# Forgetting attention: high probabilities by high, ones and low values in one 129-column product

## The chip, the core and the metric

The kernel runs on one core of a Trainium2 chip. The core has a matrix engine (TensorE, PE in the profile), a vector engine (VectorE, DVE), a scalar engine (ScalarE, ACT), GpSimd (POOL) and a sync engine (SP) that issues DMAs. The metric is the device time of one execution in microseconds, the median over several runs. Each profile is one execution, recorded by the hardware profiler.

## The reference

One decoder layer over 2048 positions of width 1024. Two mixers share a normalised input and one input projection: forgetting attention (8 heads of 64) and a sliding-window attention. Their gated outputs go through one output projection, a norm and a residual. What the change touches is the last line of the forgetting attention:

```python
def one_block(args):
    qb, cb, n = args
    s = jnp.einsum('bhqd,bhkd->bhqk', qb, kh, preferred_element_type=jnp.float32) * scale
    s = s + cb[..., None] - cum[:, :, None, :]
    ...
    s = jnp.where(causal, s, -jnp.inf)
    p = jax.nn.softmax(s, axis=-1)
    return jnp.einsum('bhqk,bhkd->bhqd', p.astype(vh.dtype), vh)
```

All of it is float32. The kernel reaches that accuracy with float16 products by splitting numbers into a high part and a low part, each float16. A product of two split numbers is then three matmuls: high by high, high by low, low by high.

## The kernel before

**Stages.** First the modulation, the norm, the transposition of the input and the sliding-window mixer with their projections (to about 480 us of the span). Then the forgetting attention (about 480 to 1025 us), with the remaining projections and, in its last head, the first part of the output projection between its steps. Then the rest of the output projection.

**Steps of the forgetting attention.** For each of 8 heads (`hd`) the queries are taken in 4 chunks of 512 (`ci`), and for each chunk the keys in pairs of 128-blocks up to the diagonal. One pair is a `Step`; there are 2, 4, 6 and 8 of them for the four chunks, 20 a head, 160 in all. A step has these parts, each a method:

- `scores` (L1286): PE computes the transposed scores of both key blocks into the PSUM tile `sta`, of which there is one buffer (`ps_st`, L1153). Two matmuls to each block (L1294, L1295), one more on the diagonal (L1297).
- `exp32` (L1299): ACT takes the exponential of `sta` to float32 (L1301).
- `high` (L1303): ACT copies that to float16, the high part of the probabilities (L1305).
- `low` (L1307): DVE subtracts, which gives the low part (L1308).
- `pv` (L1310): PE multiplies probabilities by values into the PSUM tile `poa`, of which there is one buffer (`ps_po`, L1154). For each key block and each 128-query block `u` at or below the diagonal there are three matmuls with the probabilities as weights: high by high values and ones (65 columns, L1318), high by low values (64 columns, L1320), low by high values and ones (65 columns, L1321). The values lie in `vt` as 64 high columns, a column of ones, and 64 low columns (`VW` = 129). The column of ones yields the sum of the probabilities. All of a chunk's steps accumulate in one `poa`.
- With the chunk's last step, `pv` ends in an eviction, 32 in all: DVE takes the reciprocal of the sums (L1325), multiplies (L1327), and SP's queue stores the result to DRAM (`o_d`, L1328), from where the output projection loads it in the last head.

**Order.** It is written out by hand in the loop at L1575 to L1636, and each engine's queue runs in that order. Step s issues its exponential, the low part of step s−1, the first half of other work (`todo`), its high part, the scores of step s+1, then `pv` of step s−2 (`PV_LAG` = 2), and the second half of other work. That other work is projections (L317 in units of three 512-column matmuls), and row maxima for the next head: PE computes scores again (L1245) into one of five rotating PSUM banks `bk`, and DVE reduces them (L1248, on the diagonal L1250). Some of it is put off by a tick or more (`after`), such as ACT's evictions of projections (L361, L1028) and DVE's gate multiply (L357). Splits of weights into high and low (L255 on ACT, L261 on DVE) run there too.

In particular ACT's queue has, in this order around an eviction: the high part of step s, then the exponential of step s+1. DVE's queue has the work ticked off in step s, the eviction's two instructions, then row maxima and the low part of step s.

Elsewhere in the kernel, L335 multiplies the input by value weights in 128-column matmuls with a weight load each, L340 and L767 are ACT's evictions of values from PSUM, L771 is DVE's.

Of the kernel before, what the change touches and what calls it, by code (L numbers as in the profile page):

```python
# [10 lines left out]
F32 = mybir.dt.float32  # L11
# [3 lines left out]
AF = mybir.ActivationFunctionType  # L15
ALU = mybir.AluOpType
AX = mybir.AxisListType

P = 128
# [12 lines left out]
LIFT_A = 3.0 * math.log(2.0)  # L32
XA, XB, XC = 2.0 ** 15, 2.0 ** 6, 2.0 ** -5
XM, XR, VW = 66, 69, 129
LW = 72
TWO_PI = 2.0 * math.pi
OFF_QA, OFF_KA, OFF_VA, OFF_FA, OFF_ZA = 0, 512, 1024, 1536, 1544
# [4 lines left out]
def hybrid_layer(  # L42
# [17 lines left out]
    V, A, G, PE, SP = nc.vector, nc.scalar, nc.gpsimd, nc.tensor, nc.sync  # L60
# [20 lines left out]
    def sm(n, tag):  # L81
        return small.tile([P, n], F32, tag=tag, name=tag)
# [97 lines left out]
    def bank(hold=False):  # L180
        n = next(n for n in order_ if n not in held)
        order_.remove(n)
        order_.append(n)
        if hold:
            held.add(n)
        return n
# [241 lines left out]
    start = ExitStack()  # L428
# [229 lines left out]
    def open_fox():  # L658
# [5 lines left out]
        vt = fx["vt"] = fxv.tile([P, NB, 8, VW], F16, name="vt")  # L664
        fx["lk"] = fxv.tile([P, LW], F16, name="lk")
        fx["lq"] = [fxv.tile([P, LW], F16, name=f"lq{n}") for n in range(2)]
        fx["cst"] = cst = fxv.tile([P, XR], F16, name="cst")
# [169 lines left out]
    class Pair:  # L837
# [62 lines left out]
        def pv(self):  # L900
            j, i = self.j, self.i
            po = ps_pv.tile([P, 4, 64], F32, tag="pv", name="pob")
            for e, (i_, k0, nk) in enumerate(self.blocks):
                for h in range(2):
                    for b in range(nk):
                        for n, (pp_, vv) in enumerate(((0, 0), (0, 1), (1, 0))):
                            PE.matmul(po[:, 2 * e + h, :], self.ptt[:, pp_, self.at[e] + h * nk + b, :],  # L907
                                      vb[:, k0 + b, self.g, 64 * vv:64 * vv + 64],
                                      start=(b == 0 and n == 0), stop=(b == nk - 1 and n == 2))

            def out_():
                on = onp.tile([P, 2, P], F32, tag="on", name="on")
                V.tensor_tensor(on[:].rearrange("p e (h d) -> p (e h) d", h=2), po[:],
                                self.rinv[:].unsqueeze(2).broadcast_to([P, 4, 64]), op=ALU.mult)
                G.dma_start(o_d[i // 4][(i % 4) * P:(i % 4 + 2) * P, (4 + j) * P:(5 + j) * P]
                            .rearrange("(e p) c -> p e c", p=P), on[:])

            after(1, out_)
# [231 lines left out]
    def fox_pool(name, bufs, **kw):  # L1150
        return fox.enter_context(tc.tile_pool(name=name, bufs=bufs, reuse_waits="tile", **kw))

    ps_st = fox_pool("ps_st", 1, space=PSUM)  # L1153
    ps_po = fox_pool("ps_po", 1, space=PSUM)  # L1154
# [44 lines left out]
    def ext_rows(cols, w, places):  # L1199

        px = bk[bank()][:]
        PE.matmul(px[0:LW, 0:P], cols, identh[:], start=True, stop=True)
        rw = fxr.tile([48, P], F16, tag="rw", name="rw")
# [8 lines left out]
    vt, lk, lq = fx["vt"], fx["lk"], fx["lq"]  # L1212
# [63 lines left out]
    class Step:  # L1276
# [33 lines left out]
        def pv(self):  # L1310
            hd, ph = self.hd, self.ph
            if self.first:
                self.po_[0] = ps_po.tile([P, 4, 65], F32, tag="po", name="poa")
            po = self.po_[0]
            for n, (b, u0, o) in enumerate(self.blocks):
                for u in range(u0, 4):
                    pq = slice(o + (u - u0) * P, o + (u - u0 + 1) * P)
                    PE.matmul(po[:, u, :], ph[:, 0, pq], vt[:, b, hd, 0:65],  # L1318
                              start=(self.first and n == 0 and u == 0), stop=False)
                    PE.matmul(po[:, u, 0:64], ph[:, 0, pq], vt[:, b, hd, 65:VW], start=False, stop=False)  # L1320
                    PE.matmul(po[:, u, :], ph[:, 1, pq], vt[:, b, hd, 0:65], start=False,  # L1321
                              stop=(self.last and n == len(self.blocks) - 1))
            if self.last:
                rinv = sm(4, "a_ri")
                V.reciprocal(rinv[:], po[:, :, 64])  # L1325
                on = op_.tile([P, 4, 64], F32, tag="ona", name="ona")
                V.tensor_tensor(on[:], po[:, :, 0:64], rinv[:].unsqueeze(2).broadcast_to([P, 4, 64]), op=ALU.mult)  # L1327
                SP.dma_start(o_d[self.ci][:, hd * 64:(hd + 1) * 64].rearrange("(u p) d -> p u d", p=P), on[:])  # L1328

        po_ = {}  # L1330
# [213 lines left out]
    with tc.manual_schedule():  # L1544
# [30 lines left out]
        for s, stp_ in enumerate(steps):  # L1575
            hd, r = divmod(s, NS)
# [105 lines left out]
```

## Time and profile before

| what | value |
|---|---|
| median of 3 runs | 1194.2 us (1192.35 to 1195.01) |
| span of the profiled execution, first to last instruction | 1188.7 us |
| mean granted PE clock in it | 0.993 |
| PE busy | 1147.3 us, 97% of the span |
| DVE busy | 914.1 us, 77% |
| ACT busy | 665.9 us, 56% |
| probabilities by values, three matmuls | 1088 each |
| evictions of it (reciprocal, multiply) | 32 each |

The profiled execution is a separate one from the timed runs; of its time the span is what the profile shows, and it lies 5.5 us below the median.

How to read the profile: an engine's busy time is the time in which at least one of its instructions runs. Matmuls are pipelined, so their busy times overlap and the mean duration of one is not the distance between two. A group's row gives source line, engine, operation, output and inputs, shape and count, then busy time in us, the mean duration of one in ns, then the engine's idle time just before its instructions, and what ended it. A timeline row gives the start in us from the span's start, the duration in us, the instruction, and in brackets the engine's idle time before it with what ended that.

### The profile page before, as it was taken

The numbers are of one execution on the slowest core, as the hardware profiler recorded it, in microseconds if no ns is written. First come the engines' busy times: TensorE is split into PE (matmuls) and PEld (weight loads), VectorE is DVE, ScalarE is ACT, GpSimd is POOL, SyncE is SP. The second block draws the span as 40 slices with busy tenths as digits, with TensorE's granted clock in tenths as the row PEclk, the third lists the DMA queues.
The fourth block names the chain that finished last, engine by engine and source line by source line (L and its number), as shares of the span: only waits on it lengthen the run. The fifth ranks groups of instructions, "written<-read, shape, count | busy, mean of one in ns | idle before, by whom it ended". The sixth has DMA issues, their size and how long they took to land.

```text
span 1188.7 us, 27244 instructions
## 1 busy us (share of the span) xinstructions
PE 1147.3 (97%) x10853; PEld 693.6 (58%) x10853; DVE 914.1 (77%) x2263; ACT 665.9 (56%) x1102; POOL 115.2 (10%) x231
## 2 busy tenths in 40 slices
PE   5899999999999998999999999999999999999997
PEld 2475556765558976555555555555555555555554
DVE  7876678687776748688888889887888887766665
ACT  2784345464655521476766667666666778433332
POOL 2000112212121211001000101001000000000000
PEclk9899999999999999999999999999999999999999
DMA  9745433314223322413325322212311345455642
GB/s 333 277 121 87 84 89 99 61 59 109 83 70 88 58 63 63 65 50 95 68 70 72 102 63 60 50 48 71 48 42 39 92 127 176 147 171 184 198 167 96
DMA packets 87579, 120.22 MB, mean 101 GB/s; under 512 B 27508, under 2 KB 63388, under 8 KB 87452
## 3 DMA queue, kind: packets, MB, share of 16 engines
q1 hardware_dynamic: 76184, 85.69, 24.4%
q0 software_dynamic: 10832, 32.50, 13.2%
q8 instruction: 85, 1.39, 0.6%
q14 instruction: 42, 0.34, 0.1%
q10 hardware_dynamic: 436, 0.28, 0.1%
HBM read 71.04 MB, written 25.18 MB: 81 GB/s over the span
## 4 chain that ended last, share of the span: by engine, by line
PE 79%; DVE 10%; DMA 6%; issue 2%; ACT 2%; SPq 1%; DVEq 0%; ACTq 0%
PE bk L317 29%; PE bk L1489 13%; PE bk L335 7%; PE sta L1295 4%; PE sta L1294 4%; PE bk L1245 4%; PE poa L1320 2%; PE poa L1321 2%; PE poa L1318 2%; DMA wa<-in_w_ada_dram 2%; PE pxb L888 2%; PE pss L855 2%; PE pob L907 2%; DVE a_m L1248 1%; PE bk L1410 1%
## 5 line engine op out<-in xcount | busy, mean ns | idle before, releaser
L1301 ACT ACTIVATE p<-sta,lift,scl_qk 128x1024 f32<-128x1024 f32 (+2 forms) x160 | 172.0, 1075 | 143.7 <-PE sta L1295 88.2
L317 PE MATMUL bk<-hT,wh_qk 128*128 128x512 f16 x768 | 195.3, 380 | 0.0
L1248 DVE TENSOR_REDUCE a_m<-bk 128x1 f32<-128x512 f32 x192 | 130.5, 686 | 55.2 <-PE bk L1245 54.0
L1308 DVE TENSOR_TENSOR pha<-p,pha 128x1024 f16<-128x1024 f32 (+2 forms) x160 | 169.1, 1057 | 0.2 <-ACT pha L1305 0.2
L1489 PE MATMUL bk<-wohl,oz 128*128 128x512 f16 x744 | 167.0, 379 | 0.7 <-DVE oz L1438 0.7
L1305 ACT ACTIVATE pha<-p 128x1024 f16<-128x1024 f32 (+2 forms) x160 | 148.1, 926 | 5.4 <-PE poa L1321 0.7
L1489 PEld LDWEIGHTS <-oz 128*128 128x128 f16 x744 | 71.9, 99 | 79.4 <-DVE oz L1438 2.8
L317 PEld LDWEIGHTS <-wh_qk 128*128 128x128 f16 x768 | 72.5, 98 | 78.2 <-issue 6.6
L1321 PE MATMUL poa<-vt,pha 128*128 128x65 f16 x1088 | 116.1, 192 | 1.4 <-DVE pha L1308 1.2
L1318 PE MATMUL poa<-vt,pha 128*128 128x65 f16 x1088 | 116.5, 193 | 0.5 <-DVE ona L1327 0.4
L1320 PE MATMUL poa<-vt,pha 128*128 128x64 f16 x1088 | 116.5, 194 | 0.0
L1245 PE MATMUL bk<-T 66*128 66x512 f16 (+2 forms) x320 | 110.2, 350 | 3.1 <-DVE a_m L1248 3.0
L1294 PE MATMUL sta<-T 128*128 128x512 f16 (+1 forms) x320 | 110.9, 346 | 2.5 <-ACT p L1301 2.4
L1318 PEld LDWEIGHTS <-pha 128*128 128x128 f16 x1088 | 101.5, 96 | 15.1 <-DVE ona L1327 1.5
L1295 PE MATMUL sta<-T 69*128 69x512 f16 (+1 forms) x320 | 109.8, 348 | 0.0
L1320 PEld LDWEIGHTS <-pha 128*128 128x128 f16 x1088 | 100.9, 97 | 11.4
L1321 PEld LDWEIGHTS <-pha 128*128 128x128 f16 x1088 | 100.8, 99 | 1.8 <-DVE pha L1308 1.7
L317 PE MATMUL bk<-hT,wh_za 128*128 128x512 f16 x384 | 99.7, 378 | 0.0
L335 PE MATMUL bk<-wh_va,hT 128*128 128x128 f16 x1536 | 90.7, 219 | 0.0
L335 PEld LDWEIGHTS <-hT 128*128 128x128 f16 x1536 | 87.5, 98 | 4.7 <-issue 2.1
L317 PE MATMUL bk<-hT,wh_zb 128*128 128x512 f16 x384 | 88.9, 379 | 0.0
L317 PE MATMUL bk<-hT,wh_qb 128*128 128x512 f16 x384 | 87.4, 379 | 0.0
(498 smaller groups left out, 1860.4 us busy)
## 6 DMA issues: line engine op xcount, KB each, us to landing
hT<-in_x_dram SPq DMA_DIRECT2D x20, 512.0 KB
wa<-in_w_ada_dram SPq DMA_DIRECT2D x16, 512.0 KB
z_d<-tz POOLq DMA_DIRECT2D x32, 256.0 KB, 2.9
T<-stq SPq DMA_DIRECT2D x64, 128.0 KB
T<-o_d SPq DMA_DIRECT2D x16, 512.0 KB
T<-z_d SPq DMA_DIRECT2D x16, 512.0 KB
out_dram<-hT SPq DMA_DIRECT2D x15, 512.0 KB
xt<-in_x_dram SPq DMA_DIRECT2D x12, 512.0 KB
```

The costliest lines, as they stand in the source:

```text
L317: PE.matmul(ps, whl[:, a, k, :], hT[ci][:, b, k, :], start=(k == 0 and n == 0), stop=(k == KT - 1 and n == 2))
L335: PE.matmul(ps[:, u * P:(u + 1) * P], hT[ci][:, a, k, u * P:(u + 1) * P], whl[:, b, k, :], start=(k == 0 and n == 0), stop=(k == KT - 1 an ...
L1245: PE.matmul(mx[:, :w], T[0:XM, 0, i * P:(i + 1) * P], T[0:XM, 2, pc * CH:pc * CH + w], start=True, stop=True)
L1294: PE.matmul(self.st[:, o:o + w], T[:, 3, kb_], T[:, 1, qc], start=True, stop=False)
L1295: PE.matmul(self.st[:, o:o + w], T[0:XR, 2, kb_], T[0:XR, 0, qc], start=False, stop=not diag)
L1301: A.activation(self.p32[:, :self.w], self.st[:, :self.w], AF.Exp, scale=scl[f"qk{self.hd}"][:], bias=lift[:])
L1305: A.activation(self.ph[:, 0, :self.w], self.p32[:, :self.w], AF.Copy)
L1308: V.tensor_tensor(self.ph[:, 1, :self.w], self.p32[:, :self.w], self.ph[:, 0, :self.w], op=ALU.subtract)
L1318: PE.matmul(po[:, u, :], ph[:, 0, pq], vt[:, b, hd, 0:65], start=(self.first and n == 0 and u == 0), stop=False)
L1320: PE.matmul(po[:, u, 0:64], ph[:, 0, pq], vt[:, b, hd, 65:VW], start=False, stop=False)
L1321: PE.matmul(po[:, u, :], ph[:, 1, pq], vt[:, b, hd, 0:65], start=False, stop=(self.last and n == len(self.blocks) - 1))
L1489: PE.matmul(py, self.hl[:, i, k, :], w_slot(8 * j + k)[:, cc], start=(k == 0 and m_ == 0), stop=(k == KT - 1 and m_ == 2))
```

## The change

For query blocks `u` = 0, 1, 2 the products of the high probabilities with the high values and ones and with the low values become one product of 129 columns, which leaves its low 64 columns in columns of their own; block 3 keeps its three products. The PSUM tile grows from 260 to 452 float32 columns (three times 129 and 65), within one bank. At the eviction ACT copies the low columns of three blocks to SBUF, DVE adds the high columns to them, multiplies block 3 out of PSUM, and multiplies the three others in SBUF.

```diff
--- before.py
+++ after.py
@@ -32,6 +32,7 @@
 LIFT_A = 3.0 * math.log(2.0)
 XA, XB, XC = 2.0 ** 15, 2.0 ** 6, 2.0 ** -5
 XM, XR, VW = 66, 69, 129
+PO_W = 3 * VW + 65
 LW = 72
 TWO_PI = 2.0 * math.pi
 OFF_QA, OFF_KA, OFF_VA, OFF_FA, OFF_ZA = 0, 512, 1024, 1536, 1544
@@ -1310,21 +1311,28 @@
         def pv(self):
             hd, ph = self.hd, self.ph
             if self.first:
-                self.po_[0] = ps_po.tile([P, 4, 65], F32, tag="po", name="poa")
+                self.po_[0] = ps_po.tile([P, PO_W], F32, tag="po", name="poa")
             po = self.po_[0]
             for n, (b, u0, o) in enumerate(self.blocks):
                 for u in range(u0, 4):
                     pq = slice(o + (u - u0) * P, o + (u - u0 + 1) * P)
-                    PE.matmul(po[:, u, :], ph[:, 0, pq], vt[:, b, hd, 0:65],
+                    c = u * VW
+                    w = VW if u < 3 else 65
+                    PE.matmul(po[:, c:c + w], ph[:, 0, pq], vt[:, b, hd, 0:w],
                               start=(self.first and n == 0 and u == 0), stop=False)
-                    PE.matmul(po[:, u, 0:64], ph[:, 0, pq], vt[:, b, hd, 65:VW], start=False, stop=False)
-                    PE.matmul(po[:, u, :], ph[:, 1, pq], vt[:, b, hd, 0:65], start=False,
+                    if u == 3:
+                        PE.matmul(po[:, c:c + 64], ph[:, 0, pq], vt[:, b, hd, 65:VW], start=False, stop=False)
+                    PE.matmul(po[:, c:c + 65], ph[:, 1, pq], vt[:, b, hd, 0:65], start=False,
                               stop=(self.last and n == len(self.blocks) - 1))
             if self.last:
                 rinv = sm(4, "a_ri")
-                V.reciprocal(rinv[:], po[:, :, 64])
+                V.reciprocal(rinv[:], po[:, 64:PO_W:VW])
                 on = op_.tile([P, 4, 64], F32, tag="ona", name="ona")
-                V.tensor_tensor(on[:], po[:, :, 0:64], rinv[:].unsqueeze(2).broadcast_to([P, 4, 64]), op=ALU.mult)
+                p3 = po[:, 0:3 * VW].rearrange("p (u c) -> p u c", u=3)
+                A.activation(on[:, 0:3], p3[:, :, 65:VW], AF.Copy)
+                V.tensor_tensor(on[:, 0:3], p3[:, :, 0:64], on[:, 0:3], op=ALU.add)
+                V.tensor_scalar(on[:, 3], po[:, 3 * VW:3 * VW + 64], rinv[:, 3:4], None, op0=ALU.mult)
+                V.tensor_tensor(on[:, 0:3], on[:, 0:3], rinv[:, 0:3].unsqueeze(2).broadcast_to([P, 3, 64]), op=ALU.mult)
                 SP.dma_start(o_d[self.ci][:, hd * 64:(hd + 1) * 64].rearrange("(u p) d -> p u d", p=P), on[:])
 
         po_ = {}
```

## The prediction, made before the changed kernel ran

> **What bounds the kernel now.** I read the page first.
>
> ```profile
> span 1188.7 us, 27244 instructions
> PE 1147.3 (97%) x10853; PEld 693.6 (58%) x10853; DVE 914.1 (77%) x2263; ACT 665.9 (56%) x1102; POOL 115.2 (10%) x231
> PE 79%; DVE 10%; DMA 6%; issue 2%; ACT 2%; SPq 1%; DVEq 0%; ACTq 0%
> ```
>
> TensorE (PE) is busy 97% of the span and holds 79% of the chain that ended last. The change touches only the forgetting-attention steps, which run from about 480 to 1025 us, so I asked for that stage in windows. The columns are window, its length, and the busy time of PE, PE's weight loads, VectorE (DVE), ScalarE (ACT) and GpSimd, then the granted clock.
>
> ```profile
> 500.00:600.00 100.00, 99.60 (x1043) 58.13 (x1042) 87.74 (x202) 69.29 (x81) 8.64 (x14) 1.00 0.35 81
> 700.00:800.00 100.00, 99.35 (x1013) 57.48 (x1011) 87.95 (x201) 67.57 (x78) 7.26 (x12) 1.00 0.25 59
> 900.00:1000.00 100.00, 95.90 (x1041) 57.20 (x1040) 83.27 (x166) 77.51 (x97) 1.63 (x3) 1.00 0.38 114
> ```
>
> PE hardly rests, at full clock. DVE is the second engine, 83 to 88% busy; ACT has a quarter to a third of its time free. So in this stage a nanosecond taken from PE counts, and any wait put in front of PE counts too. What PE waits for today stands in the groups of instructions (busy total, mean ns, then the idle time before them and who ended it):
>
> ```profile
> L1294 PE MATMUL sta<-T 128*128 128x512 f16 (+1 forms) x320 | 110.9, 346 | 2.5 <-ACT p L1301 2.4
> L1245 PE MATMUL bk<-T 66*128 66x512 f16 (+2 forms) x320 | 110.2, 350 | 3.1 <-DVE a_m L1248 3.0
> L1318 PE MATMUL poa<-vt,pha 128*128 128x65 f16 x1088 | 116.5, 193 | 0.5 <-DVE ona L1327 0.4
> L1321 PE MATMUL poa<-vt,pha 128*128 128x65 f16 x1088 | 116.1, 192 | 1.4 <-DVE pha L1308 1.2
> L1301 ACT ACTIVATE p<-sta,lift,scl_qk 128x1024 f32<-128x1024 f32 (+2 forms) x160 | 172.0, 1075 | 143.7 <-PE sta L1295 88.2 <-PE sta L1297 46.0 <-DVE pha L1308 3.3
> L1325 DVE RECIPROCAL a_ri<-poa 128x4 f32<-128x4 f32 x32 | 5.7, 177 | 5.4 <-PE poa L1321 5.3
> L1327 DVE TENSOR_TENSOR ona<-poa,a_ri 128x256 f32<-128x256 f32 x32 | 13.6, 424 | 1.1
> ```
>
> PE waits under 8 us in these four groups. ACT, in contrast, sits idle 143.7 us in front of the exponential at L1301: it waits for scores. That spare time is what the change spends.
>
> **Part 1: the matmuls.** Of 1088 products (query block u against key block b) each has three matmuls. Every pair of key block and query group contains u = 3 once: (4+8+12+16) × 8 heads = 320. For the other 768 the separate 64-column low product goes, and the 65-column one becomes 129 columns. Matmuls are pipelined, so the 193 ns of one is latency; the price is the distance between starts. From the timeline:
>
> ```profile
> 562.40 0.19 PE L1318 MATMUL poa<-vt,pha 128*128 128x65 f16 x1
> 563.05 0.38 PE L1245 MATMUL bk<-T 66*128 66x512 f16 x1
> 209.97 5.53 PE L335 MATMUL bk<-wh_va,hT 128*128 128x128 f16 x96
> ```
>
> Between the first two rows lie the 21 products of one burst (seven query blocks, three each): 0.65 us / 21 = 31.0 ns per narrow matmul, weight load included. The third row is 96 matmuls of 128 columns, each with its own weight load: (5.53 − 0.22) / 95 = 55.9 ns, so 129 columns cost about 56.3. A pair of narrow ones is 62, the wide one 56.3: 5.7 ns × 768 = 4.4 us saved. No row shows a 129-column product followed by a narrow one with new weights. The floor is pure column time: 55.9/128 = 0.44 ns a column makes 56.3 for the pair too, so 0 saved. I take 3.5, nearer the upper end, because that end rests on this very loop.
>
> A rule speaks against it. The Trainium skill ("TensorE: Matmul & The Clock Gate", Back-to-back issue gap) says that a sustained stream of weight load and matmul runs at about 81 ns for 128 columns. By it the wide product would lose 19 ns against its pair, 14.6 us in all. The trace's 55.9 ns, with weight loads, contradicts it.
>
> **Part 2: the eviction, 32 times.** Today DVE takes the reciprocal (177 ns) and one 256-column multiply (424 ns). The new sequence is reciprocal on DVE, a 192-column copy out of PSUM on ACT, a 192-column add on DVE, a 64-column multiply, a 192-column multiply. In the built program ACT's copy waits on DVE's semaphore at exactly the count which the reciprocal sets, and DVE's add waits for the copy. So it is a relay DVE, ACT, DVE, and ACT's queue is in order: behind the copy stands the next step's exponential (L1301).
>
> ```profile
> L340 ACT ACTIVATE vt<-bk 128x512 f16<-128x512 f32 x16 | 9.5, 596 | 17.5 <-PE bk L335 17.4
> L767 ACT ACTIVATE vb<-bk 128x128 f16<-128x128 f32 x16 | 3.6, 288 | 3.7 <-PE bk L759 3.7
> L771 DVE SCALAR_TENSOR_TENSOR vb<-bk,vb 128x128 f16<-128x128 f32 x16 | 3.9, 282 | 0.0
> ```
>
> The copy: 288 ns at 128 columns and 596 at 512 give 339 at 192. DVE: 192 columns out of PSUM lie between 282 (128) and 424 (256), 353; 64 columns between 177 (4) and 282 (128), 230; the last multiply, all in SBUF, has no row of its size: at least the 177, at most the 353, I take 300. With three handoffs of 0.04 us (the shortest from a product's end to the reciprocal, below) and the wait for the copy, DVE is held 1.5 us instead of 0.60, so 0.9 × 32 = 29 us more of DVE.
>
> Now the path. What is late next is the exponential, and behind it PE's scores: the score tile has one buffer, so L1294 of the following step can't start before L1301 has read it. Three of the 31 evictions that have a step behind them (the first, the worst, the last); the first row of each is the tile's last product, and it ends 0.19 later:
>
> ```profile
> 500.26 0.19 PE L1321 MATMUL poa<-vt,pha 128*128 128x65 f16 x1
> 500.22 1.10 ACT L1301 ACTIVATE p<-sta,lift,scl_qk 128x896 f32<-128x896 f32 x1 [1.72 <-PE sta L1297]
> 500.76 0.17 DVE L1325 RECIPROCAL a_ri<-poa 128x4 f32<-128x4 f32 x1
> 501.87 0.27 PE L1294 MATMUL sta<-T 128*128 128x256 f16 x1
> ...
> 599.87 0.19 PE L1321 MATMUL poa<-vt,pha 128*128 128x65 f16 x1
> 599.82 1.21 ACT L1301 ACTIVATE p<-sta,lift,scl_qk 128x1024 f32<-128x1024 f32 x1 [0.27 <-PE sta L1295]
> 602.50 0.18 DVE L1325 RECIPROCAL a_ri<-poa 128x4 f32<-128x4 f32 x1
> 602.28 0.38 PE L1294 MATMUL sta<-T 128*128 128x512 f16 x1
> ...
> 999.97 1.20 ACT L1301 ACTIVATE p<-sta,lift,scl_qk 128x1024 f32<-128x1024 f32 x1 [0.37 <-PE sta L1295]
> 1000.01 0.19 PE L1321 MATMUL poa<-vt,pha 128*128 128x65 f16 x1
> 1000.24 0.18 DVE L1325 RECIPROCAL a_ri<-poa 128x4 f32<-128x4 f32 x1 [0.81 <-PE poa L1321]
> 1001.98 0.38 PE L1294 MATMUL sta<-T 128*128 128x512 f16 x1
> ```
>
> Today the exponential starts 0.24 us before the products' end. In the changed order it starts after reciprocal (0.18), handoff (0.04), copy (0.34) and ACT's own turn (0.03): with r, the lag of the reciprocal behind the products' end, that is r + 0.59 after it. So it is r + 0.83 late. The slack is from the exponential's end to the next L1294, less 0.05 for the handoff. First: r = 0.31, late 1.14, slack 0.55 − 0.05, so PE stalls 0.64. Worst: r = 2.44 because DVE still had a split, a mask and a gate multiply queued ahead; late 3.27, slack 1.25 − 0.05, stall 2.07. Last: r = 0.04, late 0.87, slack 0.81 − 0.05, stall 0.11. The same subtraction for all 31 (r averages 0.54, from 0.04 to 2.44; the slack 0.81, from 0.05 to 1.26) gives stalls at 22, together 20.6 us. ACT is free when its copy may start in 30 of the 31, as the idle time in brackets shows in these three.
>
> The bounds of this term come from r, which the other DVE work sets. Were DVE always at hand (r = 0.04), the same sum would be 7 us; were every reciprocal 0.9 later, since DVE carries that much more, 47. I keep the measured lags: the evictions lie 6 to 29 us apart, DVE is idle some 13%, and a stalled PE gives DVE time to catch up.
>
> The PSUM tile also comes free later, about r + 1.25 after the products' end instead of r + 0.63. The next first product (L1318) stands behind the stalled scores, and in none of the 31 would it wait longer than these, so this adds nothing; without that cover it is 2 us at five tiles. The low-part subtraction (L1308) and the row maxima (L1248), which free PE's banks, are queued on DVE behind the relay and come up to 0.9 us later; PE waits 1.2 and 3.0 us for them today. I add 1 us. The output DMA on SP's queue starts 0.9 us later; its data is first read in the last head, several steps on, so nothing.
>
> **Sum.** 20.6 − 3.5 + 1 = +18.1 on the profiled span of 1188.7, so 1206.8. The median of the runs shown is 5.5 above that span (what lies around it); I carry the 5.5 over: 1212.
>
> **Rivals.**
> *Hidden relay, faster.* The copy fits into ACT's idle time and the scores never notice; what is left is the matmul saving, 1194.2 − 4.4 = 1190. For it: ACT's 143.7 us idle at L1301, and ten reciprocals that followed the products within 0.05 us. Against it: that idle time ends with the scores, at the very moment at which the copy takes the engine; it decides for this rival only where r + 0.83 stays under the slack, and that is 9 tiles of 31. The Trainium skill ("PSUM — Partial Sum Buffer", Terms) adds that two engines may not be in one PSUM bank at once, so the copy couldn't run beside the reciprocal either; no run here shows it.
> *DVE becomes the bound.* 29 us more at 83 to 88% load, and the lags grow at every tile: up to 47 − 3.5 = +43, 1237; halfway 1224. For it: the lags already reach 2.44. Against it: the distance between evictions.
> *Wide matmuls slow.* At 81 ns the first term is +14.6 instead of −3.5: 1230. The 96 matmuls at 55.9 ns leave it little.
> *Nothing changes.* It needs a stall sum of about 3 us, under the lower bound of 7.
>
> **How the numbers follow.** Relay stall 0.72; hidden 0.09; DVE bound 0.14; slow wide matmul 0.02; no change 0.03. A measurement here tells about 0.2% (2.4 us) from no change: faster 0.09, within 0.03, slower 0.88. The forecast's own range runs from half of the stalls to half as much again plus 2, 1202 to 1224; to leave out no more than two in ten I widen it towards the DVE case: 1201 to 1227.
>
> **What would show it.** The changed profile should have the wide product at 56 ns distance; ACT's copy near 0.34 us starting just behind the reciprocal; idle time of PE at the scores, released by the exponential, up from 2.4 to some 20 us; and DVE idle 0.4 us in front of each add. If that idle time stays under 7 us the relay is hidden; if it shows at L1245 behind the row maxima instead, DVE is the bound. I would be wrong in sign if the scores did not wait at all.

## The result, and the profile after

The changed kernel takes 1214.6 us, median of four runs (1211.5 to 1215.2), the kernel before on the same chip 1193.5; the ratio is 1.017, 95% interval [1.016, 1.019]. So it became 1.7% slower, about 21 us. Line numbers are one higher in the changed kernel from L35 on, and those behind the edit by more: the scores are L1295 and L1296, the exponential L1302, the reciprocal L1329, ACT's copy L1332, the add L1333.

Span, engines' busy times and the chain of the page after:

```profile
span 1212.5 us, 25747 instructions
PE 1152.7 (95%) x10085; PEld 693.8 (57%) x10085; DVE 925.5 (76%) x2327; ACT 671.3 (55%) x1134; POOL 114.8 (9%) x231
PE 71%; DVE 16%; DMA 6%; ACT 4%; issue 3%; SPq 0%; DVEq 0%; ACTq 0%
```

PE has 768 instructions fewer. The chain has handed 8 points of its share from PE to DVE and ACT. A run's time lies 1.7 us above its span here (1214.2 and 1212.5 for the profiled one). The spans of the two first profiles differ by 23.8 us: 2.8 before the stage, 0.7 behind it, and 20.3 in the attention stage, from the first score matmul to the end of the last product (543.3 us before, 563.6 after). What lies before the stage is no effect of the change: the kernels are the same up to there, and over all profiles here the stage begins anywhere from 477 to 482 us. The same windows as before (the last two columns are the DMA engines' share and GB/s):

```profile
500.00:600.00 100.00, 97.19 (x868) 56.12 (x867) 87.53 (x205) 67.52 (x84) 8.69 (x15) 1.00 0.35 77
700.00:800.00 100.00, 96.92 (x847) 55.23 (x846) 88.39 (x205) 65.68 (x81) 7.80 (x13) 1.00 0.24 56
900.00:1000.00 100.00, 92.47 (x866) 54.38 (x865) 81.83 (x178) 69.94 (x92) 1.62 (x3) 1.00 0.28 78
```

PE rests 3% of the first two stretches, where it rested under 1%, and 7.5% of the third, where it rested 4%. DVE is no busier than it was. The groups of instructions say what PE rests for:

```profile
L1302 ACT ACTIVATE p<-sta,lift,scl_qk 128x1024 f32<-128x1024 f32 (+2 forms) x160 | 171.7, 1073 | 91.2 <-PE sta L1296 48.9 <-PE sta L1298 34.1 <-DVE pha L1309 2.6
L1295 PE MATMUL sta<-T 128*128 128x512 f16 (+1 forms) x320 | 111.5, 348 | 17.6 <-ACT p L1302 17.3
L1246 PE MATMUL bk<-T 66*128 66x512 f16 (+2 forms) x320 | 110.2, 350 | 3.3 <-DVE a_m L1249 3.0 <-DMA T<-stq 0.2
L1333 DVE TENSOR_TENSOR ona<-poa,ona 128x192 f32<-128x192 f32 x32 | 11.4, 358 | 12.7 <-ACT ona L1332 12.7
L1335 DVE TENSOR_TENSOR ona<-ona,a_ri 128x192 f32<-128x192 f32 x32 | 11.1, 348 | 0.0
L1332 ACT ACTIVATE ona<-poa 128x192 f32<-128x192 f32 x32 | 10.6, 330 | 67.0 <-DVE a_ri L1329 66.9
L1334 DVE TENSOR_SCALAR ona<-poa,a_ri 128x64 f32<-128x64 f32 x32 | 8.8, 275 | 0.0
```

The wait for the exponential in front of the scores went from 2.4 to 17.3 us. ACT's idle time in front of the exponential fell by 52.5 us, and 66.9 us of idle time appeared in front of the copy, ended by the reciprocal: the copy now takes the place in ACT's queue where the exponential used to wait. It uses nothing that the reciprocal makes: both read `poa`, and the one written first goes first. The longest wait of the scores, in the timeline:

```profile
842.18 0.19 PE L1325 MATMUL poa<-vt,pha 128*128 128x65 f16 x1
842.60 1.21 DVE L222 TENSOR_REDUCE w_mx<-wr_qk 128x1 f32<-128x1024 f32 x1
843.73 0.68 DVE L1249 TENSOR_REDUCE a_m<-bk 128x1 f32<-128x512 f32 x1
844.33 0.17 DVE L1329 RECIPROCAL a_ri<-poa 128x4 f32<-128x4 f32 x1
844.53 0.33 ACT L1332 ACTIVATE ona<-poa 128x192 f32<-128x192 f32 x1 [4.13 <-DVE a_ri L1329]
844.76 1.20 ACT L1302 ACTIVATE p<-sta,lift,scl_qk 128x1024 f32<-128x1024 f32 x1
846.01 0.38 PE L1295 MATMUL sta<-T 128*128 128x512 f16 x1 [1.96 <-ACT p L1302]
```

The last product ends at 842.37. DVE still has a weight maximum and a row maximum to take, so the reciprocal comes 1.96 us later; copy, exponential and scores follow one behind the other, and PE stands idle for 1.96 us. That idle time has a second price. The same windows' columns, for three stretches of 3.4 us about it:

```profile
843.10:846.50 3.40, 1.44 (x8) 0.61 (x7) 3.00 (x8) 1.94 (x3) 0.57 (x1) 1.00 0.22 51
846.50:849.90 3.40, 3.40 (x23) 1.92 (x22) 1.50 (x4) 2.81 (x3) 0.00 (x0) 0.50 0.15 39
849.90:853.30 3.40, 3.40 (x25) 1.75 (x24) 2.88 (x4) 0.00 (x0) 0.00 (x0) 1.00 0.00 0
```

The stretch with the stall has PE busy for 1.44 of 3.40 us; in the next one the granted clock is 0.50, then full again. In this stage the profile after has 10.2 us at half clock, the profile before none.

### The profile page after: what moved, and what is told of

Its sections match the earlier page's. It is cut to its first block, busy times and chain, and to the rows that moved or that the text cites. A ratio compares the mean times of both kernels' runs of the same rounds, so it can differ in the third digit from the quotient of the medians.

```text
span 1212.5 us, 25747 instructions
## 1 busy us (share of the span) xinstructions
PE 1152.7 (95%) x10085; PEld 693.8 (57%) x10085; DVE 925.5 (76%) x2327; ACT 671.3 (55%) x1134; POOL 114.8 (9%) x231
## 4 chain that ended last, share of the span: by engine, by line
PE 71%; DVE 16%; DMA 6%; ACT 4%; issue 3%; SPq 0%; DVEq 0%; ACTq 0%
PE bk L318 26%; PE bk L1497 12%; PE bk L336 7%; PE sta L1295 4%; PE sta L1296 4%; PE poa L1321 3%; PE bk L1246 3%; DVE a_m L1249 3%; DVE pha L1309 3%; DMA wa<-in_w_ada_dram 2%; PE pxb L889 2%; PE poa L1325 2%; PE pss L856 2%; PE pob L908 2%; ACT p L1302 2%
## 5 line engine op out<-in xcount | busy, mean ns | idle before, releaser
L1302 ACT ACTIVATE p<-sta,lift,scl_qk 128x1024 f32<-128x1024 f32 (+2 forms) x160 | 171.7, 1073 | 91.2 <-PE sta L1296 48.9
L1295 PE MATMUL sta<-T 128*128 128x512 f16 (+1 forms) x320 | 111.5, 348 | 17.6 <-ACT p L1302 17.3
L1325 PE MATMUL poa<-vt,pha 128*128 128x65 f16 x1088 | 114.6, 194 | 1.4 <-DVE pha L1309 1.4
L1321 PE MATMUL poa<-vt,pha 128*128 128x129 f16 (+1 forms) x1088 | 114.3, 214 | 0.0
L1296 PE MATMUL sta<-T 69*128 69x512 f16 (+1 forms) x320 | 110.5, 350 | 0.0
L1321 PEld LDWEIGHTS <-pha 128*128 128x128 f16 x1088 | 99.8, 98 | 14.1 <-issue 0.3
L1325 PEld LDWEIGHTS <-pha 128*128 128x128 f16 x1088 | 97.1, 99 | 14.0 <-DVE pha L1309 1.9
L1251 DVE CUSTOM_DVE_ANT_0 bk<-bk,cmask 128x128 f32<-128x128 f32 (+3 forms) x128 | 62.5, 495 | 4.1 <-PE bk L1246 3.9
L1507 ACT ACTIVATE yj<-bk,w_sw 128x512 bf16<-128x512 f32 x31 | 21.3, 687 | 79.5 <-DVE hT L1506 79.3
```

What stands on the lines that cost most here:

```text
L1295: PE.matmul(self.st[:, o:o + w], T[:, 3, kb_], T[:, 1, qc], start=True, stop=False)
L1296: PE.matmul(self.st[:, o:o + w], T[0:XR, 2, kb_], T[0:XR, 0, qc], start=False, stop=not diag)
L1302: A.activation(self.p32[:, :self.w], self.st[:, :self.w], AF.Exp, scale=scl[f"qk{self.hd}"][:], bias=lift[:])
L1321: PE.matmul(po[:, c:c + w], ph[:, 0, pq], vt[:, b, hd, 0:w], start=(self.first and n == 0 and u == 0), stop=False)
L1325: PE.matmul(po[:, c:c + 65], ph[:, 1, pq], vt[:, b, hd, 0:65], start=False, stop=(self.last and n == len(self.blocks) - 1))
```

## The experiments

Theories. *Relay*: the loss is ACT's copy, which waits for DVE's backlog and holds up the exponential. *Rival A*: the 129-column product is slow. *Rival B*: DVE's longer eviction is what costs. Ratios are to the kernel before, run beside each.

**Each half alone.** The first kernel keeps the wide products and takes relay and add away, so it leaves out the low term of three blocks; the second keeps the narrow products and the new eviction.

```diff
 e1: wide products, eviction on DVE alone
-A.activation(on[:, 0:3], p3[:, :, 65:VW], AF.Copy)
-V.tensor_tensor(on[:, 0:3], p3[:, :, 0:64], on[:, 0:3], op=ALU.add)
...
+V.tensor_tensor(on[:, 0:3], p3[:, :, 0:64], rinv[:, 0:3]..., op=ALU.mult)
 e2: narrow products
-PE.matmul(po[:, c:c + w], ph[:, 0, pq], vt[:, b, hd, 0:w], ...)
+PE.matmul(po[:, c:c + 65], ph[:, 0, pq], vt[:, b, hd, 0:65], ...)
+PE.matmul(po[:, l:l + 64], ph[:, 0, pq], vt[:, b, hd, 65:VW], ...)   # l = c + 65 for u < 3
```

> The wide products alone: the low columns are computed into their own columns but not added (blocks 0 to 2 of each chunk lose the term high probabilities by low values), and the eviction is all on DVE (reciprocal, 192-column multiply and 64-column multiply out of PSUM), so no copy on ACT and no relay. Relay theory (the slowdown is the exponential queued behind ACT's copy, which waits for DVE's reciprocal): PE's wait for the exponential at the scores falls back to 2 to 3 us, and only the matmul saving of 2 to 4 us is left: 1189 to 1192 us against 1193.5 before. Rival A (the 129-column product is slow): stays above 1205. Rival B (extra DVE work per eviction is what costs): DVE carries 0.22 us more per eviction instead of 0.8, so about a quarter of the loss stays, some 1198.

> The new eviction alone: three narrow products as before, the low ones of blocks 0 to 2 into their own columns, then the reciprocal, ACT's copy, the add and the two multiplies as in the change. Relay theory: the whole loss and no matmul saving, the changed kernel's 1214.6 plus 2 to 4: 1216 to 1219; waits for the exponential at the scores about 17 us. Rival A (slow wide product): near before, under 1200.

Measured: the wide products alone 1.0009 [0.9997, 1.0021], the eviction alone 1.0170 [1.0149, 1.0191]. The score groups, first of the one and then of the other:

```profile
L1295 PE MATMUL sta<-T 128*128 128x512 f16 (+1 forms) x320 | 110.9, 346 | 2.6 <-ACT p L1302 2.5
```

```profile
L1295 PE MATMUL sta<-T 128*128 128x512 f16 (+1 forms) x320 | 111.4, 348 | 17.2 <-ACT p L1302 16.8
```

The whole loss is in the eviction; rival A falls. But the wide product's gain, expected at 2 to 4 us, isn't in the time at all: the first kernel comes out slower than expected, and the second, without the gain, is no slower than the change.

**What in the eviction.** The third kernel has DVE make the copy, so DVE is held about as long and ACT is left alone; the fourth puts ACT's copy ahead of the reciprocal, so it waits for PE and not for DVE; the fifth makes the copy twice.

```diff
 e3
-A.activation(on[:, 0:3], p3[:, :, 65:VW], AF.Copy)
+V.tensor_copy(on[:, 0:3], p3[:, :, 65:VW])
 e4
-V.reciprocal(rinv[:], po[:, 64:PO_W:VW])
 A.activation(on[:, 0:3], p3[:, :, 65:VW], AF.Copy)
+V.reciprocal(rinv[:], po[:, 64:PO_W:VW])
 e5
 A.activation(on[:, 0:3], p3[:, :, 65:VW], AF.Copy)
+A.activation(on[:, 0:3], p3[:, :, 65:VW], AF.Copy)
```

> The change with the low columns copied by DVE instead of ACT: the same DVE hold per eviction (about 1.5 us, the copy now in it), but nothing in ACT's queue. Relay theory: the wait for the exponential falls back to 2 to 3 us; the PSUM tile comes free 0.6 us later, worth up to 2 us of waits at five tiles; matmul saving kept: 1190 to 1195. Rival B (DVE load): as slow as the change, 1212 or more, with the waits at the row maxima or at the low part.

> The change with ACT's copy ahead of the reciprocal in the program, so that the copy waits for PE's last product and DVE's reciprocal for the copy: ACT's copy no longer waits for DVE's backlog. Relay theory with the lag r as the price: the exponential is 0.51 us late at every eviction instead of r + 0.68, which by the slacks measured before stalls PE 1.5 us in all instead of 17 to 18, and without long stalls the clock isn't halved in the stage: 1190 to 1195. If the copy's own time on ACT is the price rather than the lag, most of the loss stays, 1206 or more. Rival B (DVE load): unchanged, 1212.

> The change with ACT's copy made twice in a row. Relay theory: the exponential starts another 0.30 us late at each of the 31 evictions; by the slacks measured before, the scores' stalls grow from 17.9 to 24.5 us, so 6 to 8 us over the change: ratio 1.022 to 1.025 to before (the change: 1.017). Rival (the order around the evictions or the clock costs, not the time ACT is held): 1.017 to 1.018.

Measured: 1.0038 [1.0026, 1.0050], 1.0019 [1.0007, 1.0032], 1.0252 [1.0238, 1.0266]. The waits of PE for the exponential (total us, times, longest), one kernel each in this order:

```profile
PE sta L1295 <- ACT p L1302: 1.9, 4, 0.7
```

```profile
PE sta L1295 <- ACT p L1302: 3.7, 7, 1.0
```

```profile
PE sta L1295 <- ACT p L1302: 25.3, 27, 2.3
```

With the copy off ACT, or on ACT but not behind the reciprocal, the wait is back near its 2.4 us and so is most of the time. Neither gets below the kernel before: 1190 to 1195 us against 1193.5 were expected, at most 1.0013, and both missed that on the slow side. In the fourth kernel it is the reciprocal that waits for the copy (9.8 us at 13 evictions), so the order in which the two are written decides who waits. Rival B is good for about a quarter of the loss (1.0038 against 1.0173). The second copy adds 8.0 us of this wait, where the subtraction over the 31 slacks said 6.6, and the ratio goes up by 0.008, some 9 us. So the price is the lag of the reciprocal, and the copy's length on top of it.

**Taking the exponential out of the relay.** Three kernels issue the next step's exponential ahead of ACT's copy: with the rest as in the change, with the copy also ahead of the reciprocal, and the latter in heads 0 to 6 with head 7 as before.

```diff
 e6 (e7: copy ahead of reciprocal too; e8: e7, but head 7 as before)
+if self.nxt:
+    self.nxt.exp32()
 A.activation(on[:, 0:3], p3[:, :, 65:VW], AF.Copy)
```

> The change with the next step's exponential issued ahead of ACT's copy, all else in its order. Relay theory: the exponential is no longer late, and PE's wait for it at the scores falls to 2 to 4 us; DVE's add now waits for the exponential as well as the copy, up to 1.4 us after the products' end, which keeps the PSUM tile 0.5 to 1 us longer: ratio 0.998 to 1.004. Rival B (DVE held longer is what costs): DVE is held more than in the change, so 1.017 or more.

> As before, and ACT's copy also ahead of the reciprocal, so the relay has one handoff less. Relay theory: as the run before or a little less, ratio 0.997 to 1.003; at the end of head 6 PE is 1 to 2 us ahead of before, as in the run with the wide products alone, and loses that in the last head, where the load of the first outputs sets the pace.

> The run before for heads 0 to 6, and for head 7 the three narrow products and the old eviction. If the last head's loss came from the longer eviction there, the 1 to 2 us won by the end of head 6 stay: ratio 0.998 to 0.999. If the loads of the last head set its end whatever the eviction, the ratio is 1.000 to 1.001, as with the wide products alone.

Measured: 1.0084 [1.0070, 1.0098], 1.0056 [1.0043, 1.0069], 1.0033 [1.0020, 1.0046]: all three miss their ranges on the slow side. The wait for the exponential is down to 2.1 to 3.0 us, as expected, but other waits came. In the second of the three, from 470 to 1030 us:

```profile
PE poa L1329 <- DVE pha L1313: 2.1, 3, 1.0
PE bk L1424 <- DMA T<-o_d: 1.9, 1, 1.9
PE poa L1325 <- DVE ona L1340: 1.5, 2, 1.0
PE bk L1503 <- DVE oz L1452: 1.3, 1, 1.3
```

PE waits for the PSUM tile, for the low part, and in the last head for loads and splits. A copy behind the exponential makes DVE wait longer: 22.8 us in front of the add in the first of the three, 12.7 in the change, and 26.7 us in front of the reciprocal in the second. What DVE does next is late. So holding DVE isn't free; it was only small beside the relay. It isn't the whole of the three misses either, as the table below shows: most of it is lost in the last head. The third has the old code there, and yet it is 0.8 us behind the kernel before at the end of head 6 and 3.6 at the end of head 7. Their profiles also have 10.2, 3.4 and 3.4 us of the stage at half clock.

**Where the matmul gain went.** The first of the next two has the wide products without relay and add in heads 0 to 6, with head 7 exactly as before. The second is the kernel before, unchanged.

> The wide products alone (low columns of blocks 0 to 2 not added), in heads 0 to 6 only; head 7 exactly as before. PE should again be 1.7 us ahead of before at the end of head 6. If the loss in the last head came from the longer eviction or the wide product there, the lead stays and the ratio is 0.998 to 0.999; if the loads of the last head set its end, the lead is gone by its ninth step and the ratio is 1.000 to 1.001.

> The kernel before, unchanged, on this chip, for a second profile: ratio 0.999 to 1.001. If the 2 us which every variant loses against before at step 148 (ninth step of the last head) are a matter of the one profile they are compared with, this profile is also 2 us later there than the first; if they come from the wide product or the eviction, it agrees with the first within 0.5 us.

Measured: 1.0003 [0.9993, 1.0012] and 1.0000 [0.9990, 1.0010]. In the timeline, the exponentials of step 0, step 147 and step 148, first before:

```profile
480.66 1.10 ACT L1301 ACTIVATE p<-sta,lift,scl_qk 128x896 f32<-128x896 f32 x1 [4.95 <-PE sta L1297]
974.76 1.20 ACT L1301 ACTIVATE p<-sta,lift,scl_qk 128x1024 f32<-128x1024 f32 x1
978.87 1.19 ACT L1301 ACTIVATE p<-sta,lift,scl_qk 128x1024 f32<-128x1024 f32 x1
```

and in the ninth experiment:

```profile
479.03 1.10 ACT L1302 ACTIVATE p<-sta,lift,scl_qk 128x896 f32<-128x896 f32 x1 [4.95 <-PE sta L1298]
971.47 1.20 ACT L1302 ACTIVATE p<-sta,lift,scl_qk 128x1024 f32<-128x1024 f32 x1
977.12 1.19 ACT L1302 ACTIVATE p<-sta,lift,scl_qk 128x1024 f32<-128x1024 f32 x1
```

From step 0 to step 147 before takes 494.10 us, the ninth experiment 492.44: 1.66 us ahead. One step later it is 498.21 and 498.09: the lead is gone, though head 7 is the old code. The second profile of the kernel before agrees with the first within 0.02 us at all of these, so this is no accident of one profile. It is much the same in the other kernels. How far the exponentials lie behind the kernel before, in us, all counted from step 0 (head 6 ends with step 139, head 7 with step 159):

| kernel | step 139 | step 147 | step 148 | step 159 |
|---|---|---|---|---|
| the change | 13.9 | 15.5 | 18.4 | 20.3 |
| first, wide products alone | −1.8 | −1.8 | 0.3 | 0.2 |
| second, eviction alone | 16.5 | 18.1 | 19.2 | 19.5 |
| fourth, copy ahead of reciprocal | −0.5 | −0.5 | 2.3 | 2.4 |
| seventh, exponential and copy ahead | 0.8 | 1.7 | 4.3 | 6.0 |
| ninth, wide products in heads 0 to 6 | −1.8 | −1.7 | −0.1 | 0.5 |

So the gain is there through seven heads: 1.8 us with the wide products alone, and some 2.5 us between the eviction alone and the change. The step behind step 147 takes it away, and in the fourth kernel that one step is more than its whole loss. The seventh was expected to be 1 to 2 us ahead at the end of head 6; it is 0.8 behind. What took the lead, in the waits of the ninth from 960 to 1025 us:

```profile
DVE T L1442 <- DMA T<-z_d: 3.6, 1, 3.6
```

This is the gate multiply of the first output block (L1419 before), in DVE's queue in the middle of the last head. It needs a load of gates, which stands on SP's queue behind the load of the head outputs (L1402, L1404 before), and that one waits for the last head's first output store to land. The chain, first before and then in the ninth:

```profile
967.92 0.38 SPq L1328 DMA_DIRECT2D o_d<-ona  x1
969.97 0.33 SPq L1402 DMA_DIRECT2D T<-o_d  x1
970.51 0.37 SPq L1404 DMA_DIRECT2D T<-z_d  x1
976.49 1.29 DVE L1419 TENSOR_TENSOR T<-bk,T 128x512 f32<-128x512 f32 x2 [2.03 <-PE bk L1410]
```

```profile
964.62 0.38 SPq L1331 DMA_DIRECT2D o_d<-ona  x1
967.72 0.33 SPq L1425 DMA_DIRECT2D T<-o_d  x1
968.26 0.37 SPq L1427 DMA_DIRECT2D T<-z_d  x1
974.74 1.29 DVE L1442 TENSOR_TENSOR T<-bk,T 128x512 f32<-128x512 f32 x2 [3.58 <-DMA T<-z_d]
```

Before, DVE waits here for PE's transposes and not for the load. In the ninth the store starts 1.67 us earlier, counted from step 0, so the lead does reach the chain; but the load of gates is only 0.62 us earlier and the multiply 0.12. From the store to the load behind it 3.10 us pass instead of 2.05, and from the gate load to the multiply 6.48 instead of at most 5.98. So the lead went because these transfers took longer, with the wide products in the last head (first experiment) or without (ninth).

Why they took longer was not tested. The traces show one thing that goes with it: in all nine kernels with wide products a 16 KB packet of DMA queue q8, which the page calls "instruction", moves between that store and that load, and these lie 3.1 to 3.8 us apart; in the three runs with narrow products only, none does, and it is 2.0 to 2.1. PE has fewer instructions with the wide products, and that queue fewer packets (79 or 80 against 85), so they may fall at other places in the run. The slower gate load isn't explained by this: it is as slow in the second experiment, where no such packet meets the store.

## Why the prediction was right, point by point

- **Sign and size.** 1212 was forecast with 1201 to 1227; 1214.6 came. The relay was the likeliest case, and the two halves run apart show it as the cause.
- **Relay stalls, 20.6 us.** From the start of the instruction ahead of them on PE to their own start, the scores behind the 31 evictions take 17.5 us longer than before, at 21 of them (22 forecast). The lag r held: 0.63 us on average against 0.54. The term was 3.1 us too large, mostly because ACT starts the exponential about 0.10 us before the copy's end (844.76 against 844.86), where I had charged 0.03 after it; with that put right the same subtraction gives 17.9.
- **Prices.** Copy 330 ns (339), add 358 (353), 64-column multiply 275 (230), last multiply 348 (300); DVE held 1.39 us from the reciprocal's start to the last multiply's end (1.5).
- **Matmul saving, 3.5 us.** The distance was right: PE's busy time in these products, one row of windows each, before and in the first experiment (the second and third numbers are the length and PE's time),

```profile
490.00:1024.00 534.00, 126.55 (x3264) 19.26 (x64) 1.00 0.32 74
```

```profile
480.00:1060.00 580.00, 123.41 (x2496) 23.20 (x96) 1.00 0.34 83
```

  differ by 3.1 us. The step that failed is "in this stage a nanosecond taken from PE counts". It holds up to the last head and not in it: seven of eight heads should give 2.7 us, and 1.8 to 2.5 are there at the end of head 6, but the run with the wide products alone ends level.
- **Output store, "several steps on, so nothing".** Wrong as a reason: in the last head its landing releases the loads which the gate multiply waits for. That chain also takes part in the change's own loss. From step 147 to step 148 the change takes 6.99 us where before takes 4.11, and PE waits there behind the gate multiply, not only behind the relay:

```profile
997.34 1.29 DVE L1427 TENSOR_TENSOR T<-bk,T 128x512 f32<-128x512 f32 x2 [4.50 <-DMA T<-z_d]
998.66 1.06 ACT L1431 ACTIVATE zj<-T 128x1024 bf16<-128x1024 f32 x1 [3.24 <-DVE T L1427]
999.86 0.39 PE L1435 MATMUL bk<-w_mx,ones 128*128 128x1 f32 x2 [2.19 <-ACT zj L1431]
```

- **Row maxima and low part, +1.** They stayed at 3.0 us and went from 1.2 to 1.4.
- **"At full clock".** Not foreseen: 10.2 us of the stage at half clock, 3.41 behind the stall at 846 us and 6.83 right behind the wait at 999.86. If PE did half its work in them, they cost 5.1, an estimate and at most that. In the profile, 17.5 + 5.1 − 3.1 makes 19.5 of the stage's 20.3 us, but that leaves out the 2.19 us above and counts the saving in full, so the split isn't shown to be this one. Against the forecast's 18.1, the missing clock term made up for the oversized stall and the saving that never reached the end; that is partly luck.
- **5.5 us carried over.** Luck as well: the forecast of the span, 1206.8, was 5.7 us under the measured 1212.5, but the median lies only 2.1 above that span and not 5.5, so the time was missed by 2.6 alone. Of the 5.5, 1.7 is what a run's time lies above its own span; the rest was the first profile's execution being faster than the timed ones.
- **Rivals.** The hidden relay would have needed ACT's copy not to wait on DVE: the fourth experiment is that case; it is 0.5 us ahead up to step 147 and not faster at the end. DVE as the bound did not come; DVE's share is unchanged. The wide matmul isn't slow: in the first experiment the next product starts 57 ns behind it (median), and it costs no time. The Trainium skill's 81 ns for a sustained stream of 128 columns ("TensorE: Matmul & The Clock Gate", Back-to-back issue gap) doesn't hold here.

No version run beats the kernel before. The best with the whole computation is the fourth, at 1.0019; the first and the ninth, which leave the low term of three blocks out, are level.

## What to carry to other kernels

Idle time of an engine in front of an instruction isn't free to spend when it ends with the event that the critical path is waiting for: an instruction put ahead there delays the path by its own wait, and by the backlog of whichever engine it waits for. Before giving work to a second engine, look at which semaphore it waits on and what is queued behind it; here putting the copy ahead of the reciprocal took away nearly all of the loss. And a saving on the busiest engine counts only until the first point in the program that something else, here a chain of store and loads in the last head, sets in time.

## What the runs showed of the hardware

PE need not be idle for the whole of a stretch for the clock to fall. In the profiles here all 13 half-clock stretches inside the attention stage begin right after 3.4 us in which PE was busy for 0.4 to 2.2 us, such as the 1.44 of 3.40 shown above, and last 3.41 or 6.83 us. What decides isn't settled: in the same profile the 3.4 us from 607.60 on, with PE busy for 1.66 and a gap of 1.75 us in them, were followed by full clock. The Trainium skill ("TensorE: Matmul & The Clock Gate", What's actually happening) ties the half clock to at least one idle window of about 3.4 us; the length agrees, but a window with PE 42% busy was enough here.
